# Turning the convolution branch's output in VectorE's squares of 32 and through DRAM, in a hybrid encoder layer on one core

## The chip, the core and the metric

The kernel runs on one NeuronCore of a Trainium2 chip. The core has a matrix engine (TensorE; PE in the profile, its weight loads PEld), three engines for elementwise work (VectorE is DVE, ScalarE is ACT, GpSimd is POOL), and SyncE (SP), which here does nothing but issue DMAs. Sixteen DMA engines move data between DRAM and the on-chip memory SBUF. Matmul results land in PSUM, a small memory of eight banks per partition. SBUF and PSUM have 128 partitions.

Each engine takes its instructions strictly in its own order, and an instruction that waits holds up all behind it on the same engine. The metric is the device time of one execution, in microseconds (us), median over runs.

## What is computed

One encoder layer for 512 tokens of width 1024, in float32. Four token mixers work on h = RMSNorm(x), are gated and summed; then come cross-attention and a gated MLP. The change sits in mixer C:

```
c_a, c_g = split(c_u + b_glu, 2)                     # c_u: 512 columns each, from h @ w_in
yc = dwconv_causal(c_a * sigmoid(c_g), conv_dw) + conv_dw_b      # 31 taps along the tokens
yc = silu(layer_norm(yc, conv_ln_g, conv_ln_b))      # normalised over the 512 channels of a token
...
br = stack([ya, yf, yc, ys])                         # the four mixers
proj = einsum('bsnc,ncd->bsnd', br, w_branch)
mixed = sum(sigmoid(h @ w_gate + b_gate) * proj) @ w_out
```

The convolution wants channels on the partitions and tokens along each partition's row. The layer norm sums over channels, so it wants tokens on the partitions. Both the gain and bias of the norm (one value per channel) and the following product with `w_branch` want channels on the partitions again. So the 512 x 512 array is turned twice.

## The kernel before

**Weights.** The work is a list of jobs that `run_blocks` walks through. Nearly every job is a block of weights of 512 KB: SP loads it into a raw tile `wr` (L176, two buffers), ScalarE makes its high part `wh` (L190), VectorE the low part `wl` by subtraction (L191; four buffers each), and TensorE multiplies three combinations of high and low parts (`mm3`, L232). A block is 24 matmuls 512 columns wide. A raw tile is free once L191 has read it; a `wh`/`wl` pair is free once TensorE has used it.

**The order.** The jobs put work other than matmuls into a `Background` object: Python generators whose `yield cost, wait` tells how much work the step was worth and how long to hold back the next. After each job (and after four of eight channel tiles) `tick` lets the generators go on; `drain(name)` makes one finish. This sets the program order. A scheduler then orders each engine's instructions by a model of their times, keeping data dependences.

**The stretch of the change.** `c_jobs` makes the gated input `conv_u`, four tiles of 128 channels x 512 tokens. `conv_task` (one for each tile) does the 31 taps on VectorE into `conv_y` (L664). Meanwhile TensorE runs mixer D's blocks and then its gate and branch blocks (`gate_blocks(3, "d")`), then the four value blocks of mixer A (`v_jobs`), which keep four PSUM banks until the last is done (copied by L155 on ScalarE, subtracted by L156 on VectorE), then for each head a query and a key block (`qk_jobs`; copies L764 and L772, subtractions L765 and L774) with the attention in the background. The branch blocks of mixer C (`gate_blocks(2, "c")`) come from the second head on, after `bg.drain("conv")`.

**`conv_norm_task`** (L669) does the turns and the norm. For each of four tiles of 128 tokens, TensorE transposes four squares of 128 x 128 into one PSUM bank (`transpose`, L236), VectorE takes mean and variance (L679, L680), GpSimd makes the reciprocal root (L268, L271) and VectorE writes the normalised tile to `xn` in SBUF (L682). Then, for each of four tiles of 128 channels, TensorE turns `xn` back into a PSUM bank, ScalarE reads that bank twice (L693 for the affine part, L694 for tanh), VectorE multiplies (L695), and `split` writes the high and low parts (L158, L159) to `y["c"]`, which takes over the buffers of `conv_u` and `conv_y`.

Of the kernel before, what the change touches and what calls it, by code (L numbers as in the profile page):

```python
# [17 lines left out]
F32 = mybir.dt.float32  # L18
F32R = mybir.dt.float32r
AF = mybir.ActivationFunctionType  # L20
ALU = mybir.AluOpType
# [4 lines left out]
P = 128  # L26
S = 512
D = 1024
NT = S // P
# [54 lines left out]
def hybrid_layer(ctx: ExitStack, tc: tile.TileContext, a: dict, out: bass.AP):  # L84
    nc = tc.nc
    V, A, G, PE, SP = nc.vector, nc.scalar, nc.gpsimd, nc.tensor, nc.sync
# [4 lines left out]
    dram = ctx.enter_context(tc.tile_pool(name="dr", bufs=1, space=DRAM))  # L91
# [5 lines left out]
    def bank(tag=None):  # L97
        if tag is None:
            turn_of.n += 1
            tag = "av" if turn_of.shared and turn_of.n % 2 else "mm"  # L100
        return psum.tile([P, 512], F32, tag=tag, name=f"ps_{tag}", bufs=2)
# [29 lines left out]
    for i in range(8):  # L131
        n = ("wh", "wl")[i % 2]
# [3 lines left out]
        elif i < 6:  # L136
            n = ("fz_raw", "fz", "fe", "fu", "fd")[i - 1]
# [14 lines left out]
    def split(ps, hi, lo, scale=None):  # L152

        if scale is None:
            A.copy(hi, ps)  # L155
            V.tensor_tensor(lo, ps, hi.bitcast(F32), ALU.subtract)  # L156
        else:
            A.activation(hi, ps, AF.Copy if isinstance(scale, float) else AF.Identity, scale=scale)  # L158
            V.scalar_tensor_tensor(lo, ps, scale, hi.bitcast(F32), ALU.mult, ALU.subtract)  # L159
# [75 lines left out]
    def transpose(ps, x, n=P):  # L235
        PE.transpose(ps, x, ident[:n, :n])  # L236
        bg.clock += 0.107
# [26 lines left out]
    def rstd_of(pool, parts, n=1):  # L264

        m = pool.tile([P, n], F32, tag="st_m", name="st_m", bufs=4)
        r = pool.tile([P, n], F32, tag="st_r", name="st_r", bufs=4)
        G.tensor_tensor(m, parts[0], eps[:, :n], ALU.add)  # L268
        for part in parts[1:]:
            G.tensor_tensor(m, m, part, ALU.add)  # L270
        G.tensor_tensor(r, m, nhalf[:, :n], ALU.pow)  # L271
        return r
# [40 lines left out]
    def e4(dtype=F32):  # L313
        return m1p.tile([P, 2, S], dtype, tag="e", name="e", bufs=3)
# [54 lines left out]
    where, rows, par = {}, [], []  # L369
    for i, plan in enumerate(plans):  # L370
        r_t = m1p.tile([P, P], F32, tag="fbias" if i == 2 else "ck", name=f"rows{i}", bufs=2)
        n = 0
# [50 lines left out]
    def turn(t, half):  # L423
        ps = turned[t, half] = bank("av" if half else "tr")
        for k in range(4):
            keep(PE.transpose(ps[:, k * P:(k + 1) * P], y01[t][:, (half * 4 + k) * P:(half * 4 + k + 1) * P], ident))
# [62 lines left out]
    def pc(name, j=0, n=1):  # L489
        i, base = where[name]  # L490
        return par[i][:, base + j:base + j + n]
# [14 lines left out]
    half = {}  # L506
# [74 lines left out]
    def y8(dtype=F32R):  # L581
        return m2p.tile([P, 4, S], dtype, tag="y8", name="y8", bufs=2)
# [15 lines left out]
    conv_u, conv_y = y8(F32), y8(F32)  # L598
# [55 lines left out]
    conv_ends = []  # L654
# [14 lines left out]

    def conv_norm_task():  # L670
        xn = m1p.tile([P, 5, S], F32, tag="qk", name="xn", bufs=2)
        yield 0.0, 2.0
        for t in range(NT):
            ps = bank("tr")
            for j in range(4):
                transpose(ps[:, j * P:(j + 1) * P], conv_y[:, j, t * P:(t + 1) * P])
            st = m1p.tile([P, 6], F32, tag="bn6", name="bn6", bufs=2)
            mv = m1p.tile([P, 2], F32, tag="bn2", name="bn2", bufs=2)
            V.bn_stats(st, ps)  # L679
            V.bn_aggr(mv, st)  # L680
            r = rstd_of(m1p, [mv[:, 1:2]])
            V.tensor_scalar(xn[:, t], ps, mv[:, 0:1], r, ALU.subtract, ALU.mult)  # L682
            yield 1.7, 2.0
        while "d" in y:
            yield 0.0, 2.0
        yield 0.0, 2.0
        y["c"] = (y8(), y8())
        for j in range(4):
            ps = bank("tr")
            for t in range(NT):  # L690
                transpose(ps[:, t * P:(t + 1) * P], xn[:, t, j * P:(j + 1) * P])
            e = e4()
            A.activation(e[:, 0], ps, AF.Identity, bias=pc("ln_b", j), scale=pc("ln_g", j))  # L693
            A.activation(e[:, 1], ps, AF.Tanh, bias=half["ln_b"][:, j:j + 1], scale=half["ln_g"][:, j:j + 1])  # L694
            V.scalar_tensor_tensor(e[:, 0], e[:, 1], 1.0, e[:, 0], ALU.add, ALU.mult)  # L695
            split(e[:, 0], y["c"][0][:, j], y["c"][1][:, j], 0.5)
            yield 1.4, 1.0
# [364 lines left out]
    def mixer_jobs():  # L1062
        yield from c_jobs()
        yield then(lambda: bg.add(lam_task(), "lam"))
        yield from d_jobs()
        yield then(lambda: bg.add(conv_norm_task(), "conv"))
        wide = m1p.tile([P, NT, D], F32, tag="v", name="wide")
        free = iter([wide[:, i] for i in (0, 1, 2, 3) * 2])
# [674 lines left out]
```

## Time and profile before

| | |
|---|---|
| median of 3 runs | 1065.24 us (1065.16 to 1066.46) |
| profiled execution | span 1064.1 us from the first to the last instruction; the median of the runs is 1.1 us above it |
| TensorE busy | 1052.2 us of the span, at full clock throughout |
| VectorE / ScalarE / GpSimd busy | 796.6 / 497.5 / 147.8 us |
| DMA | 152.58 MB in 162108 packets, 143 GB/s over the span |
| SP's DMA queue (q1) | 152995 packets, 119.91 MB, 37.4% of the 16 engines' span |

The profile is one execution, recorded by the chip's profiler. Matmuls are pipelined: one starts before the last has ended, so the time that a matmul costs the stream is read from start to start, and not from its length. A group's row gives the line of the kernel, engine, operation, the tile written and the tiles read, the shape, the count, then the busy time and the mean in ns of one, then the idle time of the engine just before, and what ended it. A row of the timeline begins with its start, in us from the start of the span, and its length.

### The profile page before, as it was taken

Reading aid. Unit: us, or ns where it says so; the run is one execution under the profiler, and the core shown is the slowest. Engines: PE = TensorE matmul, PEld = TensorE weight load, DVE = VectorE, ACT = ScalarE, POOL = GpSimd, SP = SyncE. Lnnn points to the kernel's source line nnn. Section 1 sums busy time; section 2 is a strip of 40 time slices with the busy share of each in tenths; the row PEclk is TensorE's granted clock in tenths of the full one; section 3 lists DMA queues with packets and bytes.
Section 4 is the critical chain, followed back from the end, with each engine's and each line's share of the span. In section 5 each row is a group of like instructions: output and inputs, shape, how many; then the busy total and the mean of one; then the engine's idle time right before and its main releaser. Section 6 shows DMA issues by size and latency. Waiting matters only on the chain.

```text
span 1064.1 us, 14583 instructions
## 1 busy us (share of the span) xinstructions
PE 1052.2 (99%) x5375; PEld 895.3 (84%) x5375; DVE 796.6 (75%) x1262; ACT 497.5 (47%) x819; POOL 147.8 (14%) x249
## 2 busy tenths in 40 slices
PE   9999999999999999999999999999999999999997
PEld 8888888888888978888888899999888888888886
DVE  6999997567666357776675888786778787777796
ACT  5322222367465255645443565664333333445662
POOL 4000000000001015332110031021111211111001
PEclk9999999999999999999999999999999999999999
DMA  8954333322222242332344754225576766725672
GB/s 264 300 155 103 104 96 99 97 82 80 80 80 63 58 139 79 100 99 80 119 125 140 268 159 120 80 75 190 180 228 218 237 219 216 235 82 179 204 219 81
DMA packets 162108, 152.58 MB, mean 143 GB/s; under 512 B 5567, under 2 KB 135212, under 8 KB 162037
## 3 DMA queue, kind: packets, MB, share of 16 engines
q1 hardware_dynamic: 152995, 119.91, 37.4%
q10 hardware_dynamic: 6482, 23.21, 5.8%
q0 software_dynamic: 2560, 8.54, 2.8%
q8 instruction: 42, 0.69, 0.3%
q14 instruction: 29, 0.24, 0.1%
HBM read 133.79 MB, written 17.84 MB: 142 GB/s over the span
## 4 chain that ended last, share of the span: by engine, by line
PE 93%; issue 3%; DMA 1%; ACT 1%; DVE 1%; POOL 0%; POOLq 0%; DVEq 0%; SPq 0%; ACTq 0%
PE ps_mm L232 50%; PE ps_av L232 29%; PE ps_sc L232 7%; PE ps_tr L232 4%; PE ps_tr L236 3%; DMA wide<-in_w_out 1%; DMA ck<-crows 0%; PE ps_mm L384 0%; DMA crows<-e 0%; PE ps_sc L389 0%; DVE nt L281 0%; POOL st_r L271 0%; ACT hth L432 0%; ACT wa L412 0%; ACT wh L190 0%
## 5 line engine op out<-in xcount | busy, mean ns | idle before, releaser
L190 ACT CAST wh<-wr 128x1024 fp32r<-128x1024 f32 (+1 forms) x142 | 148.7, 1050 | 273.1 <-PE ps_mm L232 181.1
L191 DVE TENSOR_TENSOR wl<-wr,wh 128x1024 fp32r<-128x1024 f32 (+1 forms) x142 | 178.2, 1256 | 89.4 <-ACT wh L190 89.1
L232 PE MATMUL ps_mm<-hth,wh 128*128 128x512 f32 (+1 forms) x616 | 231.4, 382 | 0.6 <-DVE qk L765 0.3
L232 PE MATMUL ps_mm<-htl,wh 128*128 128x512 f32 (+1 forms) x616 | 230.2, 380 | 0.0
L232 PE MATMUL ps_mm<-hth,wl 128*128 128x512 f32 (+1 forms) x616 | 229.9, 380 | 0.0
L232 PEld LDWEIGHTS ps_mm<-hth,wh 128*128 128x128 f32 x616 | 114.1, 188 | 21.7 <-ACT hth L155 0.8
L232 PEld LDWEIGHTS ps_mm<-hth,wl 128*128 128x128 f32 x616 | 114.0, 188 | 21.1
L232 PEld LDWEIGHTS ps_mm<-htl,wh 128*128 128x128 f32 x616 | 114.2, 188 | 20.4
L232 PE MATMUL ps_av<-hth,wh 128*128 128x512 f32 (+1 forms) x328 | 122.6, 374 | 0.0
L232 PE MATMUL ps_av<-htl,wh 128*128 128x512 f32 (+1 forms) x328 | 122.5, 374 | 0.0
L232 PE MATMUL ps_av<-hth,wl 128*128 128x512 f32 (+1 forms) x328 | 122.5, 373 | 0.0
L664 DVE SCALAR_TENSOR_TENSOR y<-y,par,y 128x482 f32<-128x482 f32 (+29 forms) x120 | 83.9, 743 | 0.2
L232 PEld LDWEIGHTS ps_av<-hth,wl 128*128 128x128 f32 x328 | 61.6, 188 | 10.9
L232 PEld LDWEIGHTS ps_av<-htl,wh 128*128 128x128 f32 x328 | 61.6, 188 | 10.9
L232 PEld LDWEIGHTS ps_av<-hth,wh 128*128 128x128 f32 x328 | 61.7, 188 | 10.7
L1536 DVE TENSOR_TENSOR wl<-dw,wh 128x1024 fp32r<-128x1024 f32 x32 | 40.2, 1261 | 12.2 <-ACT wh L1535 12.0
L1535 ACT CAST wh<-dw 128x1024 fp32r<-128x1024 f32 x32 | 33.4, 1051 | 22.6 <-PE ps_tr L232 7.5
L990 POOL TENSOR_SCALAR fbias<-ck,cq 128x128 f32<-128x128 f32 (+3 forms) x32 | 27.5, 865 | 69.0 <-DVE st L996 61.8
L1484 ACT ACTIVATE th<-c 128x512 f32<-128x512 f32 x22 | 13.9, 631 | 48.5 <-DVE c L594 45.6
L155 ACT CAST pth<-ps_tr 128x512 fp32r<-128x512 f32 (+3 forms) x56 | 23.4, 448 | 22.0 <-PE ps_tr L236 21.8
L594 DVE SCALAR_TENSOR_TENSOR c<-ps_mm,par,c 128x510 f32<-128x510 f32 (+1 forms) x44 | 32.7, 744 | 0.7
L156 DVE TENSOR_TENSOR ptl<-ps_tr,pth 128x512 fp32r<-128x512 f32 (+3 forms) x56 | 27.9, 512 | 6.0 <-ACT pth L155 5.7
(471 smaller groups left out, 2105.2 us busy)
## 6 DMA issues: line engine op xcount, KB each, us to landing
wr<-in_w_up SPq DMA_DIRECT2D x44, 512.0 KB
wr<-in_w_in SPq DMA_DIRECT2D x38, 512.0 KB
wr<-in_w_gate SPq DMA_DIRECT2D x32, 512.0 KB
wp<-in_w_down ACTq DMA_DIRECT2D x22, 512.0 KB
sums<-wp ACTq DMA_DIRECT2D x22, 512.0 KB
dw<-sums SPq DMA_DIRECT2D x44, 256.0 KB
wr<-in_w_branch SPq DMA_DIRECT2D x16, 512.0 KB
wide<-in_w_out SPq DMA_DIRECT2D x12, 512.0 KB
```

The costliest lines, as they stand in the source:

```text
L155: A.copy(hi, ps)
L156: V.tensor_tensor(lo, ps, hi.bitcast(F32), ALU.subtract)
L190: order(A.copy(hi, raw[:, :n]))
L191: low.tensor_tensor(lo, raw[:, :n], hi.bitcast(F32), ALU.subtract)
L232: PE.matmul(ps, lhs, rhs, start=start, stop=stop)
L236: PE.transpose(ps, x, ident[:n, :n])
L594: ins = V.scalar_tensor_tensor(dst[:, s:], src[:, :S - s], w(k), dst[:, s:], ALU.mult, ALU.add)
L664: ins = V.scalar_tensor_tensor(dst[:, s:], src[:, :S - s], pc("conv_dw", k * 4 + j), dst[:, s:], ALU.mult, ALU.add)
L990: G.tensor_scalar(bias[:, :w], ck[j][:, :w], -1.0, cq[:, qt, head:head + 1], ALU.mult, ALU.add)
L1484: A.activation(th, c[:, 0], AF.Tanh, scale=0.5)
L1535: A.copy(hi, x)
L1536: V.tensor_tensor(lo, x, hi.bitcast(F32), ALU.subtract)
```

## The change

Both turns leave TensorE. A new inner function `turn` does each in three steps: VectorE turns every square of 32 x 32 inside a 128 x 512 tile (`V.transpose`, four instructions); SP stores the tiles to a 512 x 512 array in DRAM so that the squares land in their transposed places, with four DMAs, one for each 32 partitions, each in rows of 32 floats; and SP loads that array back into `xn`, four DMAs of 128 rows of 512 floats. The turned squares of the first turn go to `conv_u`, which the taps no longer need; those of the second to `conv_y`. The statistics and the normalisation then read `xn` in SBUF, the normalisation works in place, and ScalarE's two activations read `xn` in SBUF where they read a PSUM bank. The task waits (in program order) until all four convolution tiles are done, and its `yield` costs are other ones.

```diff
     def conv_norm_task():
         xn = m1p.tile([P, 5, S], F32, tag="qk", name="xn", bufs=2)
+        tok, chan = (dram.tile([S, S], F32, name=n) for n in ("conv_tok", "conv_chan"))
+
+        def turn(rows, squares, src):
+            for i in range(4):
+                V.transpose(squares[:, i], src[:, i])
+                yield 0.65, 0.0
+            form = rows.rearrange("(b r) (j a c) -> a r j b c", r=32, a=4, c=32)
+            for a in range(4):
+                SP.dma_start(form[a], squares[a * 32:a * 32 + 32].rearrange("r j (b c) -> r j b c", c=32))
+            yield 0.0, 4.0
+            for i in range(4):
+                SP.dma_start(xn[:, i], rows[i * P:(i + 1) * P, :])
+            yield 0.0, 5.0
+
         yield 0.0, 2.0
+        while len(conv_ends) < 4:
+            yield 0.0, 0.5
+        yield from turn(tok, conv_u, conv_y)
         for t in range(NT):
-            ps = bank("tr")
-            for j in range(4):
-                transpose(ps[:, j * P:(j + 1) * P], conv_y[:, j, t * P:(t + 1) * P])
...
-            V.bn_stats(st, ps)
+            V.bn_stats(st, xn[:, t])
...
-            V.tensor_scalar(xn[:, t], ps, mv[:, 0:1], r, ALU.subtract, ALU.mult)
-            yield 1.7, 2.0
+            V.tensor_scalar(xn[:, t], xn[:, t], mv[:, 0:1], r, ALU.subtract, ALU.mult)
+            yield 1.5, 0.0
+        yield from turn(chan, conv_y, xn)
...
         for j in range(4):
-            ps = bank("tr")
-            for t in range(NT):
-                transpose(ps[:, t * P:(t + 1) * P], xn[:, t, j * P:(j + 1) * P])
             e = e4()
-            A.activation(e[:, 0], ps, AF.Identity, bias=pc("ln_b", j), scale=pc("ln_g", j))
-            A.activation(e[:, 1], ps, AF.Tanh, bias=half["ln_b"][:, j:j + 1], scale=half["ln_g"][:, j:j + 1])
+            A.activation(e[:, 0], xn[:, j], AF.Identity, bias=pc("ln_b", j), scale=pc("ln_g", j))
+            A.activation(e[:, 1], xn[:, j], AF.Tanh, bias=half["ln_b"][:, j:j + 1], scale=half["ln_g"][:, j:j + 1])
```

In the changed kernel L676 is the square transpose, L680 the stores, L683 the loads, L693 to L696 statistics and normalisation, and L705 and L706 the two activations that were L693 and L694.

## The prediction

> **What bounds the kernel now.** I read the page's first part, then its chain, then the stretch where the turned data is made and used. Columns of the first row: busy us, share, instructions.
>
> ```profile
> PE 1052.2 (99%) x5375; PEld 895.3 (84%) x5375; DVE 796.6 (75%) x1262; ACT 497.5 (47%) x819; POOL 147.8 (14%) x249
> ...
> PE 93%; issue 3%; DMA 1%; ACT 1%; DVE 1%; POOL 0%; POOLq 0%; DVEq 0%; SPq 0%; ACTq 0%
> ```
>
> TensorE is busy 99% of the span, and the chain that ended last is 93% TensorE. So a matmul taken from its stream is worth its time, and a gap opened in that stream is paid in full. The busy time by windows says the same of the stretch that the change touches; columns: window, its length, busy us of PE, PEld, DVE, ACT, POOL, clock, DMA share, GB/s.
>
> ```profile
> 182.00:190.00 8.00, 8.00 (x41) 6.69 (x41) 4.73 (x7) 1.64 (x2) 2.41 (x6) 1.00 0.40 128
> 190.00:200.00 10.00, 10.00 (x46) 8.29 (x45) 4.81 (x8) 2.10 (x2) 1.35 (x4) 1.00 0.20 55
> 200.00:210.00 10.00, 10.00 (x50) 8.24 (x49) 3.94 (x5) 5.55 (x8) 0.00 (x0) 1.00 0.38 105
> 210.00:220.00 10.00, 10.00 (x50) 8.36 (x49) 7.78 (x11) 7.94 (x13) 1.04 (x2) 1.00 0.36 105
> ```
>
> TensorE has no gap at all there; VectorE is busy about half the time until 210, the DMA engines a third. So how early do weights arrive? VectorE's timeline (start, length, then what ended the idle time) and TensorE's:
>
> ```profile
> 173.79 0.75 DVE L664 SCALAR_TENSOR_TENSOR y<-y,par,y 128x511 f32<-128x511 f32 x1
> 174.45 1.22 DVE L191 TENSOR_TENSOR wl<-wr,wh 128x1024 fp32r<-128x1024 f32 x1
> 179.45 1.23 DVE L191 TENSOR_TENSOR wl<-wr,wh 128x1024 fp32r<-128x1024 f32 x1 [3.78 <-ACT wh L190]
> ...
> 192.02 1.22 DVE L191 TENSOR_TENSOR wl<-wr,wh 128x1024 fp32r<-128x1024 f32 x1
> ```
> ```profile
> 190.42 0.39 PE L232 MATMUL ps_av<-wh,hth 128*128 128x512 f32 x1
> ...
> 212.94 0.39 PE L232 MATMUL ps_mm<-wh,htl 128*128 128x512 f32 x1
> 213.18 1.03 PE L236 MATMUL ps_tr<-ident,xn 128*128 128x128 f32 x8
> 213.97 0.48 PE L232 MATMUL ps_mm<-hth,wh 128*128 128x512 f32 x1
> 214.28 0.39 PE L232 MATMUL ps_mm<-htl,wh 128*128 128x512 f32 x1
> ...
> 219.29 0.39 PE L232 MATMUL ps_mm<-hth,wl 128*128 128x512 f32 x1
> 219.52 0.39 PE L232 MATMUL ps_mm<-hth,wh 128*128 128x512 f32 x1
> ```
>
> The last tap of the convolution ends at 174.5. The weight block split at 174.45 is used from 190.42, so blocks are ready some 15 us ahead. A block of 24 matmuls goes at 0.227 us each (219.29 to 219.52), 5.45 us. After four value blocks come the first query block Q (213.97) and its key block K (219.52).
>
> **The change part by part.** *Removed from TensorE:* 32 transposes. In the row of eight, 213.18 to 214.28 holds eight transposes and one matmul: (1.10 - 0.227)/8 = 0.109 us each, since they are pipelined. 32 x 0.109 = **3.5 us** saved. The Trainium skill ("VectorE: DVE Perf Modes", The three transpose paths) gives a 128x128 transpose as 390 ns on TensorE; an estimate by that figure would save 12.5 us and bring my sum below to -1.4 us. The row's 0.109 speaks against it, so the trace decides.
>
> *Added on VectorE:* eight 128x512 square transposes. No such row exists; the nearest are these (mean ns after the busy time):
>
> ```profile
> L695 DVE SCALAR_TENSOR_TENSOR e<-e 128x512 f32<-128x512 f32 x4 | 2.8, 693 | 1.0 <-ACT e L694 0.6
> L679 DVE BATCH_NORM_STATS2 bn<-ps_tr 128x6 f32<-128x512 f32 x4 | 2.6, 689 | 1.1 <-PE ps_tr L236 1.1
> L682 DVE TENSOR_SCALAR xn<-ps_tr,bn,st_r 128x512 f32<-128x512 f32 x4 | 3.1, 806 | 0.8 <-POOL st_r L271 0.8
> L660 DVE TENSOR_SCALAR y<-y,par,par 128x512 f32<-128x512 f32 x4 | 2.2, 555 | 0.0
> ```
>
> I take 0.69 (from 0.55, the cheapest, to 1.4, two passes): 5.5 us, less 4 x 0.25 because the normalisation reads SBUF (L660) and not PSUM (L682). VectorE's free half hides it; only the part inside the chain below counts.
>
> *Added on DMA:* per turn, four stores of 2048 rows of 128 bytes and four loads of 128 rows of 2 KB. All are on SP's queue, which also issues each weight load. What does such a store cost? Windows with rows of 4096 bytes, before and during one 512 KB load in rows of 512 bytes, and that load's issue:
>
> ```profile
> 39.50:43.00 3.50, 3.50 (x17) 2.88 (x17) 2.57 (x4) 0.69 (x1) 0.00 (x0) 1.00 1.03 393
> ...
> 186.40:187.00 0.60, 0.60 (x4) 0.52 (x3) 0.00 (x0) 0.00 (x0) 0.00 (x0) 1.00 0.00 0
> 187.00:189.50 2.50, 2.50 (x16) 2.14 (x15) 1.38 (x3) 0.00 (x0) 0.00 (x0) 1.00 0.72 209
> ```
> ```profile
> 186.40 0.37 SPq L176 DMA_DIRECT2D wr<-in_w_in  x1
> ```
>
> Share x 16 engines x row bytes / rate: 16 x 1.03 x 4096 / 393 = 172 ns per 4 KB row; 16 x 0.72 x 512 / 209 = 28 ns per 512-byte row. A line through both gives 12.8 ns for 128 bytes. A turn has 8192 such rows, 512 on each engine. Call its stores' time X: **6.6 us** by the line, **14.4 us** if a short row costs what the nearest measured one (512 bytes) does, 29 us if each is handled twice. I take the middle of the first two, **X = 10.5**; the bounds stay for the range. A load is landed 3.1 us after its issue (0.8 to the first bytes, 2.3 of data).
>
> *What waits.* In the built program's order, VectorE's statistics of the first turn stand ahead of the split of Q's weights, SP's loads of each turn stand behind the wait for its stores, and ScalarE's first two L705/L706 pairs stand ahead of the copy that frees the last PSUM bank of the value blocks. K needs that bank. This is the chain:
>
> 1. First turn: last transpose ends near 178 (174.5 + four transposes and a weight split that moved ahead of it). First bytes 0.9 later, stores done at 178.9 + X. Behind them in the queue lie two weight loads (2.3 each), then the turned rows (0.7 to the first): 184.2 + X. Statistics start at S, the later of that and the end of the split ahead of them. Its cast (row below) waits for TensorE, which comes 16 transposes or 1.8 us earlier: 190.4 - 1.8 + 1.05 + 1.22 = 190.9. For X below 6.6 the first turn is hidden; at 10.5 it adds 3.9, so S = 194.8.
> 2. From S: four statistics, two aggregates and the POOL step (2.9), four normalisations at 0.55, four transposes at 0.69, two aggregates 0.3, a weight split 1.23: about 9.4. The squares are done at 204.2.
> 3. Second turn: a weight load issued just before delays the stores to 1.7 after that; stores done 205.9 + X = 216.4; again a weight load behind them 2.3, then two loads of rows 1.4 and the semaphore 0.2: xn's second quarter at 220.3.
> 4. ScalarE's four L705/L706 steps (L693/L694 before) at 0.78 run from the first quarter, 219.6, to 222.7; then the copy 0.59 and VectorE's subtraction 0.69 (rows below), with some 0.1 between engines. **K can start at 224.1.**
>
> ```profile
> 190.39 1.05 ACT L190 CAST wh<-wr 128x1024 fp32r<-128x1024 f32 x1 [4.69 <-PE ps_mm L232]
> ...
> 209.10 0.77 ACT L694 ACTIVATE e<-ps_tr,s_ln_b,s_ln_g 128x512 f32<-128x512 f32 x1
> ...
> 213.37 0.59 ACT L155 CAST v<-ps_mm 128x512 fp32r<-128x512 f32 x1 [0.78 <-PE ps_mm L232]
> ```
> ```profile
> 213.99 0.69 DVE L156 TENSOR_TENSOR v<-ps_mm,v 128x512 fp32r<-128x512 f32 x1 [0.67 <-ACT v L155]
> ```
>
> TensorE would want K at 219.52 - 3.5 = 216.0. Gap: **8.1 us**. In general K starts at 209.7 + X + max(0, X - 6.6).
>
> *Behind the wait* on ScalarE stand two weight casts, the other two L705/L706 pairs, three y["c"] copies and the two copies of Q's product; on VectorE their subtractions. The next query block needs Q's bank, so it waits for all of them: 2 x 1.05 + 4 x 0.78 + 5 x 0.6 = 8.2 us from the end of the copy that freed K's bank, 0.7 ahead of K's start, and one subtraction of 0.7 after. That is about 8.3 behind K's start, where K lasts 5.45: **3.0 us** more, with small waits between the engines. The weights for it are split by then.
>
> Sum: -3.5 + 8.1 + 3.0 = **+7.6 us**, on the profiled span of 1064.1: 1071.7. The median of the runs, 1065.24, is 1.1 above that span, so 1072.8, say **1073 us**. Behind 245 us every engine keeps its order; ahead of 155 us VectorE turns two squares between taps, 1.4 us that the 15 us of lead hide (without it they would be TensorE's).
>
> **Rivals.** *Hidden transfers* (faster): if a short row costs by the line or less, X is at most 6.6, the first turn is under the 190.9 bound and the second brings K to 216.3 or earlier. The copies behind K then start early enough for the 3.0 to shrink too, and nothing but the 3.5 us is left: 1061.7. For it: DMA share under 0.4 in these windows, and weights 15 us ahead. Against it: it leaves no slack for anything else in the chain. It decides at X = 6.3, counting K alone; with the 3.0 behind K, the sum turns near X = 6.7.
>
> *Short stores handled twice* (slower than the forecast): X from 20 to 29 gives K at 243 to 261, a gap of 27 to 45, in sum +27 to +45: 1092 to 1110. For it: no row of the trace shows a store to DRAM in rows this short, so nothing excludes it. The Trainium skill ("DMA: Bandwidth & Descriptors", Specifications) states that transfers below 512 B lead to a read-modify-write, which would be this mechanism; no run here shows it.
>
> *Gain and gap balance:* X of 6.7 to 7.9, 0 to +2.1: 1065.2 to 1067.4, the same.
>
> *Weights starve instead:* SP's weight loads lie behind the stores. At X = 10.5 the first load behind them lands at 191.7 and its block is needed at 205.8, so this is not the wait that decides; from X near 22 it is, and it adds nothing to K's own wait.
>
> **How the numbers follow.** Forecast (X of 7.9 to 20, 1067.4 to 1092): 0.55. Hidden: 0.20. Balance: 0.10. Handled twice: 0.15. Differences below 0.2% (2.1 us) are what a measurement of this kernel can't tell from none. So faster 0.20, same 0.10, slower 0.70. The range takes in the hidden case and the forecast up to X = 20: 1061.5 to 1092, leaving out most of the case handled twice.
>
> **What would show it.** In the profile after: TensorE without its transposes between 158 and 214 and Q started near 210.5; a gap in TensorE of some 8 us ahead of K, put down to VectorE's subtraction L156 or ScalarE's copy; DMA windows full of short packets for about 10 us twice; ScalarE's L705 released by DMA. Wrong if the stores take under 6.6 us, if the gap is ahead of Q or a value block instead, or if square transposes take several us.

## The result, and the profile after

| | before | after |
|---|---|---|
| median of 4 runs each, on one chip | 1065.23 us (1065.16 to 1066.46) | 1060.88 us (1059.94 to 1061.46) |
| ratio | | 0.9961, 95% interval 0.9945 to 0.9977 |
| profiled execution | span 1064.1 us | span 1059.7 us (a run of 1061.46 us) |

The forecast was 1073.0 us, slower; the kernel came out 4.35 us faster, below the range's end of 1061.5. It is a difference of 0.4%. In twelve further runs, beside 29 of before, the changed kernel gained less: 1062.65 against 1065.66 us, ratio 0.9982 (0.9970 to 0.9994).

The page's first line, as in the prediction: TensorE's 32 transposes are gone, 3.5 us of its busy time with them, and VectorE's share barely moves.

```profile
PE 1048.7 (99%) x5343; PEld 891.8 (84%) x5343; DVE 800.8 (76%) x1270; ACT 497.9 (47%) x819; POOL 150.8 (14%) x249
```

Next two windows of the changed kernel (window, length, busy us of PE, PEld, DVE, ACT, POOL, clock, DMA share, GB/s). They lie inside the stores of the two turns.

```profile
178.70:184.40 5.70, 5.70 (x27) 4.72 (x26) 1.49 (x2) 1.64 (x2) 0.00 (x0) 1.00 1.18 184
201.60:207.40 5.80, 5.80 (x28) 4.79 (x27) 1.82 (x2) 1.94 (x3) 0.00 (x0) 1.00 1.20 182
```

A turn stores 512 x 512 x 4 bytes = 1.049 MB. At 184 and 182 GB/s that is 5.7 and 5.8 us: this is **X**, which the prediction took as 10.5. TensorE still waits twice in this stretch. Its timeline shows where:

```profile
214.84 0.39 PE L232 MATMUL ps_mm<-hth,wl 128*128 128x512 f32 x1
215.41 0.50 PE L232 MATMUL ps_mm<-hth,wh 128*128 128x512 f32 x1 [0.19 <-DVE v L156]
...
220.76 0.39 PE L232 MATMUL ps_mm<-hth,wl 128*128 128x512 f32 x1
223.02 0.47 PE L232 MATMUL ps_mm<-hth,wh 128*128 128x512 f32 x1 [1.87 <-DVE qk L777]
```

From start to start a matmul takes 0.227 us, so the stream loses 0.57 - 0.23 = 0.34 us ahead of the first key block (K) and 2.26 - 0.23 = 2.03 us ahead of the next query block. ScalarE's timeline says why: its first L705 waits for the second turn's rows, and only behind two pairs of L705 and L706 comes the copy that frees K's bank.

```profile
211.09 0.81 ACT L705 ACTIVATE e<-xn,par 128x512 f32<-128x512 f32 x1 [2.04 <-DMA xn<-conv_chan]
...
213.23 0.80 ACT L706 ACTIVATE e<-xn,s_ln_b,s_ln_g 128x512 f32<-128x512 f32 x1
213.94 0.56 ACT L155 CAST v<-ps_mm 128x512 fp32r<-128x512 f32 x1
...
220.47 0.81 ACT L706 ACTIVATE e<-xn,s_ln_b,s_ln_g 128x512 f32<-128x512 f32 x1
221.30 0.58 ACT L776 CAST qk<-ps_mm 64x512 fp32r<-64x512 f32 x1
```

So this stretch is worth -3.5 + 0.34 + 2.03 = **-1.1 us**. TensorE's timelines, of before and of after, give it directly too, from the first matmul on `y8b`, ahead of all that the change touches, to the first scores:

```profile
134.06 0.61 PE L232 MATMUL ps_av<-y8b,wh 128*128 128x512 f32 x2
...
230.40 0.56 PE L232 MATMUL ps_sc<-qk 128*128 128x128 f32 x4
```
```profile
133.46 0.62 PE L232 MATMUL ps_av<-y8b,wh 128*128 128x512 f32 x2
...
228.56 0.56 PE L232 MATMUL ps_sc<-qk 128*128 128x128 f32 x4
```

That is 96.34 us before and 95.10 after, a difference of -1.24. The two profiled spans differ by 4.4. Some 0.6 us of that lie ahead of the change (134.06 against 133.46), where both kernels do the same. Where is the rest? In the list of what TensorE waited for, before has a line that after has not (engine, tile, line, releaser: us in total, times, longest):

```profile
PE ps_sc L232 <- DVE st L996: 2.4, 1, 2.4
```

This wait sits at 398.87, some 180 us behind the last instruction that the change touches. POOL's timelines, of before and of after, show its root: a store of 16 KB to DRAM (`crows`, the running gate sums of the decay mixer), which POOL reads back into `ck` to build the bias of the first scores.

```profile
388.39 0.57 POOL L943 DMA_DIRECT2D crows<-e  x1 [30.58 <-DVE e L942]
392.58 1.11 POOL L960 DMA_DIRECT2D ck<-crows  x2 [3.62 <-DMA crows<-e]
397.74 0.37 POOL L990 TENSOR_SCALAR fbias<-ck,cq 128x128 f32<-128x128 f32 x1 [4.04 <-DMA ck<-crows]
```
```profile
386.56 0.57 POOL L955 DMA_DIRECT2D crows<-e  x1 [30.58 <-DVE e L954]
388.97 1.11 POOL L972 DMA_DIRECT2D ck<-crows  x2 [1.84 <-DMA crows<-e]
392.67 0.37 POOL L1002 TENSOR_SCALAR fbias<-ck,cq 128x128 f32<-128x128 f32 x1 [2.59 <-DMA ck<-crows]
```

In before POOL waits 3.62 us for that store and 4.04 for the reading back, in after 1.84 and 2.59. The code there is the same. Whether this belongs to the change was the main question of the experiments.

### The profile page after: what moved, and what is told of

Read it like the earlier page. It is cut to its first block, busy times and chain, and to the rows that moved or that the text cites. A ratio compares the mean times of both kernels' runs of the same rounds, so it can differ in the third digit from the quotient of the medians.

```text
span 1059.7 us, 14546 instructions
## 1 busy us (share of the span) xinstructions
PE 1048.7 (99%) x5343; PEld 891.8 (84%) x5343; DVE 800.8 (76%) x1270; ACT 497.9 (47%) x819; POOL 150.8 (14%) x249
## 4 chain that ended last, share of the span: by engine, by line
PE 95%; DMA 1%; DVE 1%; ACT 1%; issue 0%; POOL 0%; SPq 0%; POOLq 0%; DVEq 0%; ACTq 0%
PE ps_mm L232 51%; PE ps_av L232 29%; PE ps_sc L232 7%; PE ps_tr L232 4%; PE ps_tr L236 3%; DMA xn<-conv_tok 1%; PE ps_mm L442 1%; PE ps_av L442 1%; DMA conv_chan<-y 0%; PE ps_mm L384 0%; SPq L680 0%; PE ps_sc L389 0%; DMA xn<-conv_chan 0%; DVE wl L191 0%; POOL st_r L271 0%
## 5 line engine op out<-in xcount | busy, mean ns | idle before, releaser
L232 PEld LDWEIGHTS ps_av<-htl,wh 128*128 128x128 f32 x328 | 61.6, 188 | 10.8
L155 ACT CAST pth<-ps_tr 128x512 fp32r<-128x512 f32 (+3 forms) x56 | 23.4, 448 | 22.0 <-PE ps_tr L236 21.9
```

Of the source, the lines that this page charges most:

```text
L232: PE.matmul(ps, lhs, rhs, start=start, stop=stop)
```

## The experiments

Theory: the gain is the 32 transposes at 0.109 us less the two gaps, about 1 us, and the rest is the late `crows` store, which comes and goes. Rivals: the change is worth the whole difference, or the transposes are not what it gains. "Kernel before" is run again beside each group of experiments, and ratios are to those runs.

**The kernel before again**, unchanged.

> The kernel before, unchanged, profiled a second time. In the two profiles the kernel after is 0.6 to 0.8 us ahead before the change begins, and it gets 2.45 us back at 398 us, where TensorE in the profile before waited 2.4 us for the scores of the first forgetting head (GpSimd's store of crows landed 3.6 us after its issue, in the profile after 1.8). If these 3 us are chance of one profile, this run shows a shorter wait there and a span nearer 1061.5; if they belong to the kernel's own phases, the wait of 2 to 3 us is there again and the span is 1064 again. Time in both cases 1065 if the three earlier runs are typical.

Median 1066.62 us in 10 runs, ratio 1.0004 (0.9990 to 1.0019), but the profiled run took 1062.49. In it POOL's store lands in time and TensorE waits nowhere near 398 us:

```profile
387.80 0.57 POOL L943 DMA_DIRECT2D crows<-e  x1 [30.57 <-DVE e L942]
390.20 1.12 POOL L960 DMA_DIRECT2D ck<-crows  x2 [1.83 <-DMA crows<-e]
```

Its times lie in two groups: three runs of 1062.49 to 1063.39 and seven of 1065.73 to 1068.12. The prediction's baseline was one profile of the upper group.

**The transposes put back**: the changed kernel, and 32 transposes of the identity whose results nobody reads.

```diff
             V.bn_stats(st, xn[:, t])
+            ps = bank("tr")
+            for j in range(4):
+                transpose(ps[:, j * P:(j + 1) * P], ident)
...
         for j in range(4):
+            ps = bank("tr")
+            for t in range(NT):
+                transpose(ps[:, t * P:(t + 1) * P], ident)
             e = e4()
```

> The kernel after with 32 transposes of the identity put back on TensorE, read by nobody, four for each tile of tokens and four for each tile of channels. Output unchanged. Theory: the gain is the 32 x 0.109 = 3.5 us that left TensorE; TensorE then comes to the query block 3.5 us later, the two small gaps behind it (0.35 and 2.05 us) are filled, and the time is 1.1 us above the kernel after, 1062.0, or up to 1064.5 if the wait at 398 us comes back. Rival: the gain lies in the later stretch and not in the transposes; then the time stays at 1060.9.

1065.73 us (10 runs), ratio 1.0012 (0.9995 to 1.0029): the gain is gone, so it hangs on the transposes and not on the later stretch. But the time lies above the 1062.0, or up to 1064.5, that the theory gave. Against the 0.9982 of the changed kernel's twelve runs it is 0.30%, 3.2 us; that this comes near 32 x 0.109 = 3.5 is in part chance. In the trace the two gaps are filled, as expected, but the scheduler put three of the four L155 copies behind activations of the turned rows, and a new gap opens ahead of the first query block (Q):

```profile
215.75 0.50 PE L232 MATMUL ps_mm<-hth,wh 128*128 128x512 f32 x1 [1.02 <-DVE v L156]
```

From the first matmul on `y8b` to the first scores TensorE takes 97.49 us (134.73 to 232.22), 2.4 more than in the changed kernel: the transposes and this gap, less the two that were filled. This run was also 1.3 us late ahead of the change (134.73 against 133.46). Where the other runs lose their time was not recorded.

**Each store twice**, the first copy to an array that nobody reads.

```diff
-            for a in range(4):
-                SP.dma_start(form[a], squares[a * 32:a * 32 + 32].rearrange("r j (b c) -> r j b c", c=32))
+            more = dram.tile([S, S], F32, name=rows.name + "_more")
+            form_more = more.rearrange("(b r) (j a c) -> a r j b c", r=32, a=4, c=32)
+            for to in (form_more, form):
+                for a in range(4):
+                    SP.dma_start(to[a], squares[a * 32:a * 32 + 32].rearrange("r j (b c) -> r j b c", c=32))
```

> The kernel after with each turn's squares stored twice, first to an array that nobody reads, then to the one that is loaded. Stores per turn X = 5.8 us become about 11.7. Theory (the chain of the prediction with the right X): K can start at 209.7 + 11.7 + 5.1 = 226.5, two weight loads now stand between stores and loads of the second turn, so up to 229; TensorE wants it at 215, so a gap of 11 to 14 us ahead of K and some 2 behind, time 1071 to 1075. Rival (transfers are hidden whatever they cost, within the 15 us by which weights are ahead): 1061 to 1062.

1068.29 us (10 runs), ratio 1.0023 (1.0012 to 1.0034): between the two expectations. The stores run at 173 GB/s, so X = 2.097 MB / 173 = 12.1 us:

```profile
178.50:190.00 11.50, 11.50 (x53) 9.51 (x52) 3.65 (x4) 2.01 (x3) 0.00 (x0) 1.00 1.26 173
```

For X = 12.1 the prediction's chain puts K at 227.3, in sum +10.8 us; measured is about +5.0 over the old order without the late store (1063.34, below). The scheduler put the instructions of the next stretch in another order, and TensorE waits later and in pieces, 0.33 + 1.90 + 1.06 + 1.97 = 5.3 us:

```profile
226.99 0.30 PE L232 MATMUL ps_sc<-qk 128*128 128x128 f32 x1 [0.33 <-DVE qk L789]
234.70 0.73 PE L232 MATMUL ps_sc<-qk 128*128 128x256 f32 x4 [1.90 <-DVE st L846]
236.49 1.92 PE L232 MATMUL ps_sc<-qk 128*128 128x384 f32 x4 [1.06 <-DVE st L846]
240.38 0.76 PE L232 MATMUL ps_mm<-hth,wh 128*128 128x512 f32 x1 [1.97 <-DVE qk L780]
```

Behind the third wait a window shows the granted clock (the column of 0.50):

```profile
236.49:246.20 9.71, 7.74 (x18) 5.59 (x19) 7.67 (x23) 7.04 (x20) 0.00 (x0) 0.50 0.20 55
```

At half the clock these 7.74 us of work are an estimated 3.9 us longer than at full clock, so the sum is -3.5 + 5.3 + 3.9 = +5.7, near the +5.0. The prediction's chain does not stand in this kernel: all four L155 copies come ahead of the first activation of the turned rows (210.10 against 225.97), so K waits for none of them.

**The same bytes in rows half as long**: 16384 rows of 64 bytes in a turn.

```diff
             for a in range(4):
-                SP.dma_start(form[a], squares[a * 32:a * 32 + 32].rearrange("r j (b c) -> r j b c", c=32))
+                for h in range(2):
+                    c = slice(h * 16, h * 16 + 16)
+                    SP.dma_start(form[a][..., c],
+                                 squares[a * 32:a * 32 + 32].rearrange("r j (b c) -> r j b c", c=32)[..., c])
```

> The kernel after with each store in two halves of 16 columns, so 16384 rows of 64 bytes a turn and not 8192 of 128: the same bytes in twice the rows. If a row costs a fixed part and its bytes (8 ns and 0.037 ns a byte, from the packets of 512 to 4096 bytes), 64 bytes take 10.4 ns against 12.8, X is about 9.5, K starts at 209.7 + 9.5 + 2.9 = 222, a gap of 7 us, time about 1067. If bytes alone set the price, X stays at 5.8 and the time at 1061. If rows below some size are handled twice, X is over 15 and the time over 1077.

1074.16 us (4 runs), ratio 1.0089 (1.0068 to 1.0109): none of the three times expected. The rate halves, so X doubles to 1.049 / 92 = 11.4 us, and a gap of 12.23 us opens behind K:

```profile
178.50:190.00 11.50, 11.50 (x53) 9.51 (x52) 3.15 (x4) 1.64 (x2) 0.00 (x0) 1.00 1.00 92
```
```profile
220.07 0.39 PE L232 MATMUL ps_mm<-hth,wl 128*128 128x512 f32 x1
232.69 0.47 PE L232 MATMUL ps_sc<-qk 128*128 128x128 f32 x1 [12.23 <-ACT qk L788]
```

512 rows on each engine in 5.7 us, or 1024 in 11.4, are 11.1 ns each: at these two lengths the price is by the row. For X = 11.4 the prediction's chain gives -3.5 + 9.9 + 3.0 = +9.4 us; measured is about +10.8 over the same 1063.34. That the two are near is luck. Here too all four L155 copies stand ahead of the activations, and K starts on time. The gap lies behind it, ahead of the first scores, whose copy L788 stands behind all eight activations of the turned rows. So neither this kernel nor the last tests the chain of the changed kernel with a long X: a change of the stores also changes the order.

**The changed kernel again**, beside the next three.

> The changed kernel once more, beside the next three. Theory (the gain is the 32 transposes, 3.5 us, less a gap of about 2 us behind the second turn; the wait of some 2.5 us near 398 us comes and goes between executions, whatever the kernel): ratio to the kernel before 0.996 to 0.999, between 1 and 4 us under it, with two groups of times some 2 to 3 us apart. Rival (the change itself ends the wait near 398 us, and the first result shows the whole gain): 0.995 to 0.997 in every execution, and TensorE waits nowhere near 398 us.

1062.65 us (12 runs; ten of them 1061.10 to 1063.32, two 1064.28 and 1066.07), ratio 0.9982 (0.9970 to 0.9994), span 1059.3. That is 1.1 us under the 1060.4 of the profile of before without the wait. The theory's interval holds. Of its two groups the upper one is rare here: at most those two runs of 12, where 20 of the 29 of before beside them are at 1064.5 or more. Neither of the two was profiled, so that they have the wait is not shown.

**Only the first turn** through DRAM; the turn back stays on TensorE.

```diff
...
-        yield from turn(chan, conv_y, xn)
...
         for j in range(4):
+            ps = bank("tr")
+            for t in range(NT):
+                transpose(ps[:, t * P:(t + 1) * P], xn[:, t, j * P:(j + 1) * P])
...
-            A.activation(e[:, 0], xn[:, j], AF.Identity, bias=pc("ln_b", j), scale=pc("ln_g", j))
-            A.activation(e[:, 1], xn[:, j], AF.Tanh, bias=half["ln_b"][:, j:j + 1], scale=half["ln_g"][:, j:j + 1])
+            A.activation(e[:, 0], ps, AF.Identity, bias=pc("ln_b", j), scale=pc("ln_g", j))
+            A.activation(e[:, 1], ps, AF.Tanh, bias=half["ln_b"][:, j:j + 1], scale=half["ln_g"][:, j:j + 1])
```

> Only the first turn goes through DRAM; the turn back stays 16 transposes on TensorE. Theory (transposes at 0.109 us each are the gain and the first turn is hidden): 1.75 us come off TensorE's stream, no gap ahead of Q, K or the next query block, so 1.5 to 2 us under the kernel before. Rival (the first turn costs something of its own, behind which statistics come late): the time of the kernel before or above it, with a gap of TensorE between 190 and 220 us.

1061.46 us (12 runs), ratio 0.9973 (0.9959 to 0.9987): faster than the whole change. TensorE's waits, complete, have nothing in this stretch, so the first turn is hidden:

```profile
PE ps_mm L384 <- DVE e L335: 1.3, 1, 1.3
PE ps_mm L232 <- ACT hth L155: 0.2, 1, 0.2
```

4.2 us under the kernel before is more than the 1.5 to 2 that the theory gave; here too the wait near 398 us is absent.

**Only the second turn**, with the first on TensorE as before.

```diff
...
-        while len(conv_ends) < 4:
-            yield 0.0, 0.5
-        yield from turn(tok, conv_u, conv_y)
         for t in range(NT):
+            ps = bank("tr")
+            for j in range(4):
+                transpose(ps[:, j * P:(j + 1) * P], conv_y[:, j, t * P:(t + 1) * P])
...
-            V.bn_stats(st, xn[:, t])
+            V.bn_stats(st, ps)
...
-            V.tensor_scalar(xn[:, t], xn[:, t], mv[:, 0:1], r, ALU.subtract, ALU.mult)
-            yield 1.5, 0.0
+            V.tensor_scalar(xn[:, t], ps, mv[:, 0:1], r, ALU.subtract, ALU.mult)
+            yield 1.7, 2.0
```

> Only the turn back goes through DRAM; the first turn stays 16 transposes on TensorE. Theory: 1.75 us come off TensorE's stream and the gap ahead of the next query block stays (0.35 and 2.05 us in the changed kernel, since this turn's stores start at about the same time): 0 to 1.8 us under the kernel before, and the trace shows a wait on VectorE's subtraction of Q near 223 us. Rival (the gap came from the first turn's delay of the statistics): no gap, 1.75 us under the kernel before.

1068.01 us (12 runs), ratio 1.0020 (1.0004 to 1.0035): slower, and both expectations failed. All four L155 copies now stand behind three pairs of L705 and L706, so the wait falls ahead of Q and not behind K, and it is longer. ScalarE and TensorE:

```profile
207.93 0.82 ACT L705 ACTIVATE e<-xn,par 128x512 f32<-128x512 f32 x1 [5.41 <-DMA xn<-conv_chan]
...
213.13 0.56 ACT L155 CAST v<-ps_av 128x512 fp32r<-128x512 f32 x1
```
```profile
215.80 0.80 PE L232 MATMUL ps_mm<-hth,wh 128*128 128x512 f32 x1 [3.49 <-DVE v L156]
216.40 0.63 PE L232 MATMUL ps_mm<-htl,wh 128*128 128x512 f32 x1
216.82 0.63 PE L232 MATMUL ps_mm<-hth,wl 128*128 128x512 f32 x1
```

Behind this gap matmuls start 0.42 us apart in place of 0.227, and a window shows the granted clock, 0.50:

```profile
215.80:221.50 5.70, 5.70 (x13) 4.47 (x14) 4.77 (x7) 3.89 (x6) 1.04 (x2) 0.50 0.21 56
```

The window's 13 matmuls at 0.2 us too much are another 2.6 us. So the sum is -1.75 + 3.5 + 2.6 = +4.3 us against the old order without the late store (1063.34, below); measured, +4.7.

**ScalarE's work on the turned rows later**, by longer holds ahead of and inside the last loop.

```diff
-        yield 0.0, 2.0
+        yield 0.0, 26.0
...
-            yield 1.4, 1.0
+            yield 1.4, 3.0
```

> The changed kernel with ScalarE's work on the turned-back rows placed later, behind the copies that free the banks of the value blocks and of Q. Theory (the 0.35 and 2.05 us that TensorE waits ahead of K and of the next query block come from ScalarE's L705 and L706 standing ahead of those copies): both gaps go, and the kernel is about 2 us under the changed kernel, 3.5 us under the kernel before. Rival (the copies themselves or VectorE's subtractions are late, whatever stands ahead): the gaps stay, the time of the changed kernel. A third way: the later copies of the next stage move the wait behind 230 us, and the sum is the same or worse.

1074.18 us (6 runs), ratio 1.0091 (1.0075 to 1.0106): the third way. The copies moved into the first scores and probabilities of the attention, and TensorE waits there, 6.5 us of it for the probabilities, with a granted clock of 0.50 from 240 to 250 us:

```profile
PE ps_tr L236 <- DVE e L853: 6.5, 1, 6.5
PE ps_sc L232 <- ACT qk L785: 2.7, 2, 1.6
```

**The two DRAM arrays declared in the kernel before**, and not used.

```diff
         xn = m1p.tile([P, 5, S], F32, tag="qk", name="xn", bufs=2)
+        tok, chan = (dram.tile([S, S], F32, name=n) for n in ("conv_tok", "conv_chan"))
```

> The kernel before with the two DRAM tiles of the change declared and never used, every instruction and its order as before. Its point: the times of the kernel before lie in two groups, 1062.1 to 1063.8 and 1064.5 to 1068.0, the changed kernel's mostly in one. Theory (the groups come from where data lies in DRAM, which the two tiles shift; with them POOL's small store lands in time more often): most runs in the lower group, ratio about 0.998 to the kernel before. Rival (the groups come with the kernel's own timing, or by chance): the same two groups in about the same shares, ratio within 0.999 to 1.001.

1066.68 us (12 runs), ratio 1.0007 (0.9993 to 1.0021); two of 12 runs below 1064.5. The rival holds: declaring the arrays makes no difference that can be told.

**Two more profiles of the kernel before.**

> The kernel before unchanged, for one more profile. Theory (the upper group of its times is the wait near 398 us): TensorE waits about 2.4 us near 398 us if the profiled run is above 1064.5, and not if it is below 1064. Rival: the upper group has no such wait, and the time lies elsewhere.

> As the look before it: a second profile of the kernel before. Theory: a time above 1064.5 goes with a wait of about 2.4 us near 398 us, a time below 1064 with none. Rival: no such link.

1065.25 and 1066.15 us, both of the upper group, and both with the wait, of 2.0 and 1.5 us; the run with the two arrays has it as well (1.8). The lines of the first and of the second:

```profile
PE ps_sc L232 <- DVE st L996: 2.0, 1, 2.0
```
```profile
PE ps_sc L232 <- DVE st L996: 1.5, 1, 1.5
```

So in the profiles the upper group goes with this wait. Of those without a turn through DRAM four have it and one has not; of the eight with such a turn up to here none has it.

**The `crows` store on SP's queue**, in the kernel before, in the changed kernel, and in the one with the first turn only. With it the cast and the split of one weight block change their place in the order, alike in all three.

```diff
-        G.dma_start(crows, row[:8, 0])
+        SP.dma_start(crows, row[:8, 0])
```

> The kernel before with the small store of the running gate sums (crows) issued by SP and not by POOL. Theory (the upper group of its times is the late landing of that store on POOL's queue): the upper group goes, 1062 to 1064 in most runs, ratio about 0.997 to 0.998 to the kernel before. Rival (it lands late on either queue, or what follows it waits anyway): ratio 0.999 to 1.001 and the wait near 398 us is there still.

> The changed kernel with the same store issued by SP. Theory (the change itself is worth about 1.1 us in the span and 0.35 outside it, the rest of the gain is the wait near 398 us that it rarely shows): 1.0 to 2.0 us under the kernel before with this store, so its time is that of the changed kernel, 1061 to 1062.5. Rival (the change is worth 3 to 4 us without that wait too): 1058 to 1060.

> Only the first turn through DRAM and the small store on SP. Theory: 16 transposes less at 0.109 us, nothing of the second turn's gap, no wait near 398 us: about 2 us under the kernel before with that store, 1060 to 1061. Rival (the store on SP delays the weight loads behind it): a wait of TensorE on VectorE's weight split behind 390 us, and 1062 or more.

| with the store on SP | median us | ratio to the kernel before (1065.51) |
|---|---|---|
| the old order | 1063.34 (1062.33 to 1064.28, 12 runs) | 0.9983 (0.9972 to 0.9993) |
| the whole change | 1062.29 (1060.82 to 1064.50, 12 runs) | 0.9973 (0.9961 to 0.9984) |
| the first turn only | 1061.37 (1060.44 to 1062.07, 9 runs) | 0.9964 (0.9951 to 0.9978) |

The upper group is gone from the old order, and the wait is gone from the list of what TensorE waited for, complete:

```profile
PE ps_mm L384 <- DVE e L335: 1.3, 1, 1.3
PE ps_mm L232 <- ACT hth L155: 0.2, 1, 0.2
PE ps_tr L426 <- DVE nt L421: 0.2, 1, 0.2
```

This one line of another stage takes 2.2 us off the old order (1065.51 to 1063.34). Beside it the change is worth **1.05 us** (1063.34 to 1062.29), as the -1.1 us of the stretch says; the first turn alone is worth 2.0, about what its 16 transposes cost (1.75 at 0.109 us each, 1.9 at the 0.117 worked out below), and the second turn gives 0.9 back. The intervals overlap, since each holds the spread of before, but TensorE's stream says the same: from the first matmul on `y8b` to the first scores it takes 96.34 to 96.38 us in the six profiles of the old order, 95.10 to 95.34 in the three of the whole change, and 94.33 and 94.36 in the two of the first turn alone. The first turn with the store on SP is the fastest of the kernels that ran together, if 0.4 us above the 1060 to 1061 expected of it.

## Why the prediction was wrong

**The step that failed** is "I take the middle of the first two, **X = 10.5**". X was 5.7 and 5.8 us, below even the lower bound of 6.6 that the line through two row lengths gave. The middle had no reason of its own. Its upper end gave a short row the price of one of 512 bytes (28 ns), of which by the line some 20 ns go with the bytes; rows of 128 and of 64 bytes both went at 11.1 ns. The line itself was nearly right: by the prediction's formula the packets of the first window took 16 x 1.18 x 128 / 184 = 13.1 ns, where the line gave 12.8. X came out under 6.6 because the packets' times overlap, to a share of 1.18, where the bound took a share of 1.

With X = 5.8 the prediction's own formulas have no gap ahead of K and a sum of -3.5 + 3.0 = -0.5 us, 1064.7: no difference that can be told. The first four runs came out 3.8 us below even that. Some 0.6 us of this are the smaller gaps and the dearer transposes of the stretch; the late store of the baseline, with 2.4 us, is most of the rest.

What the other steps said, one by one:

- *Transposes at 0.109 us*: nearly right. From its first matmul on `y8b` TensorE comes to Q after 79.91 us in before (to 213.97) and 76.16 in after (to 209.62): 3.75 us for 32 transposes, 0.117 each. The 390 ns of the Trainium skill ("VectorE: DVE Perf Modes", The three transpose paths), which the prediction set against its own figure, are given for bf16; these tiles are float32.
- *Square transposes at 0.69, normalisation from SBUF at 0.55*: right, and hidden:

```profile
L676 DVE STREAM_TRANSPOSE y<-xn 128x512 f32<-128x512 f32 x4 | 2.6, 684 | 0.0
L696 DVE TENSOR_SCALAR xn<-xn,bn,st_r 128x512 f32<-128x512 f32 x4 | 2.1, 534 | 0.1
```

- *The first turn's statistics start at the later of 190.9 and 184.2 + X*: they started at 191.22, the last 1.08 us of it waiting for the rows. So the rows were last, and not the split of the weights, and they came 1.2 us later than 184.2 + 5.8 = 190.0. For TensorE the first turn is hidden all the same: with it alone no wait lies in this stretch.

```profile
191.22 1.41 DVE L693 BATCH_NORM_STATS2 bn<-xn 128x6 f32<-128x512 f32 x2 [1.08 <-DMA xn<-conv_tok]
```

- *K starts at 209.7 + X + max(0, X - 6.6)*: with X = 5.8 that is 215.5; it started at 215.41. For this X the chain was right to some 0.6 us (the changed kernel's profile runs that much ahead), and the term put into it was too large. That it holds for a long X is not shown.
- *3.0 us behind K*: 2.03. The prediction let it shrink to nothing if the transfers are hidden. It did not: K starts within 0.4 us of TensorE's wish, but the copies of Q's product (the last L776 at 221.30) still stand behind the other two pairs of L705 and L706, weight casts and copies for `y["c"]`.
- *Stores handled twice*: the Trainium skill ("DMA: Bandwidth & Descriptors", Specifications) states a read-modify-write for transfers below 512 B. No run shows it as a doubled price. Rows of 128 and of 64 bytes both cost 11.1 ns, less than half of the 28 ns of a 512-byte row.

The rival *hidden transfers* (chance 0.20) gave 1061.7, near the first result, but for two reasons that cancel: it left the second turn's gaps out (+2.4 us) and did not know of the late store (-2.2). By its mechanism alone, with the gaps, the sum was -1.1 us, 1064.1, which lies within the 2.1 us that the prediction calls no difference.

**A step that was missing**: the baseline's own profile had a TensorE wait of 2.4 us in its list, and the prediction took its span as given. Here such a wait hung on one DMA's landing and not on any engine's work; whoever forecasts a change of 1 us must ask whether it will be there in the next run.

**What stays open**: why a kernel with a turn through DRAM rarely shows that wait. At most two of 12 runs of the changed kernel are in the upper group, where 20 of 29 of before are. It is not the transposes (with them put back the wait is absent too, in the one profile), and not the arrays' place. In before the store's landing took 3.9 us and in the run without the wait 2.1; an instruction fetch of 16 KB lies in both stretches, so its presence alone decides nothing. These are the rows, of the profile of before and of its repetition:

```profile
q8 instruction: 1, 0.02, 2.0%
...
crows<-e POOLq DMA_DIRECT2D x1, 16.0 KB, 3.9
```
```profile
q8 instruction: 1, 0.02, 1.7%
...
crows<-e POOLq DMA_DIRECT2D x1, 16.0 KB, 2.1
```

Nothing was tried that moves the fetch.

## What to carry to other kernels

Price a DMA of many short rows by the row, from a line through two row lengths of the same trace, and not at the nearest longer row's price. Test a two-part change by its halves: here the first turn earned 2.0 us in the shadow of other work, and the second gave 0.9 of it back because its rows came just ahead of copies that TensorE needs. And look for a wait in the baseline that one late DMA makes: moving one store to another queue was worth twice the change.

## What the runs showed of the hardware

- A store to DRAM in rows of 128 or 64 bytes took 11.1 ns a row on each of 16 engines (11.8 where each store was made twice).
- A gap of 3.49 us halved TensorE's granted clock for the next 5.7 us, so the gap cost 6.1. The Trainium skill ("TensorE: Matmul & The Clock Gate", Part 1) puts the half clock behind an idle window of about 3.4 us, and this row agrees. Others do not. With each store made twice, waits of 1.90 and 1.06 us were enough for 0.50. In the second of the two further profiles of before, waits of 1.48 and 0.32 us near 398 us were enough, and the matmuls behind them start 0.43 us apart until 402; its windows, below, show means of 0.82 and 0.75. Yet 1.87 us in the changed kernel, and 2.36 and 0.31 us near 398 us in before, left the clock at 1.00. So here the length of a gap alone does not decide, and what does is open.

```profile
396.00:400.00 4.00, 2.21 (x7) 1.61 (x7) 1.34 (x6) 0.00 (x0) 1.99 (x6) 0.82 0.33 110
400.00:404.00 4.00, 4.00 (x16) 3.24 (x15) 3.02 (x9) 3.07 (x8) 2.51 (x4) 0.75 0.00 0
```

- The kernels with a turn through DRAM lie 1.7 to 1.8 us above their span, those without 2.1 (1061.1 against 1059.3, 1062.49 against 1060.4). The 0.3 us lie outside what the profile shows.
